# Spreading the first loads of a two-layer decoder over three DMA queues

## The chip, the cores and the metric

The kernel runs on one core of a Trainium2 chip. The metric is the device time of one execution in microseconds (us), as the median of several executions. Engines go by the profile's short names: PE is TensorE (PEld its weight loads), ACT is ScalarE, DVE is VectorE, POOL is GpSimd, SP is SyncE. SP, ACT and POOL can issue DMA transfers; an issue on SP or ACT is a step of that engine's instruction stream, and the transfers themselves run on 16 DMA engines that all three share.

## The reference

The input is x, 512 tokens of 1024 features in float32. Two layers follow each other, and each does this:

```python
x = x + 0.5 * swiglu(rms_norm(x, ffn1_norm[l]), ffn1_w_gate[l], ffn1_w_up[l], ffn1_w_down[l])
h = rms_norm(x, mix_norm[l])
a, g, q, k, v = jnp.split(h @ w_in[l], splits, axis=-1)
conv_out = conv_module(a, g, conv_w[l], conv_b[l], conv_norm[l])
...
x = x + jnp.concatenate([conv_out, diff_out], axis=-1) @ w_out[l]
x = x + 0.5 * swiglu(rms_norm(x, ffn2_norm[l]), ffn2_w_gate[l], ffn2_w_up[l], ffn2_w_down[l])
```

swiglu(h) is (silu(h @ w_gate) * (h @ w_up)) @ w_down with 2816 hidden features. The change concerns how x, the first gate and up weights and the layers' small parameters get into the core at the very start. None of the arithmetic is touched.

## The kernel before, in words

The activations are kept with features on the 128 partitions: x has KT = 8 feature tiles x[0] to x[7], each 128 x 512 (256 KB, and it stays on the chip through both layers). To multiply in float32 on TensorE, each operand is split into two parts, hi and lo, of the type float32r, and each product is three matmuls: hi by hi (line 163), hi of the weights by lo of x (166), lo of the weights by hi of x (167). For weights, ScalarE makes hi (line 100; for the very first piece VectorE, line 98) and VectorE makes lo (line 101). For x, a Prep object makes acth on ScalarE (line 262) and actl on VectorE (line 263), with the norm's gain, a column of the parameter tile pars[l], multiplied in; the row statistics come later, from squares on ScalarE (line 271) that GpSimd adds up (line 275).

The first stretch is written out by hand. The parameters of both layers (79.5 KB each) are issued on ScalarE's queue (line 179). Then an activation that needs nothing loads the activation table (line 184), and IDLE = 9 matmuls without use keep TensorE busy (line 187). Four weight tiles of the first feed-forward, gate and up of hidden tiles 0 and 1, are loaded in three pieces each on SP's queue, between the feature tiles that they are multiplied with: columns for feature tile 0 (64 KB), for tiles 1 to 3 (192 KB), for tiles 4 to 7 (256 KB). On SP the issues thus stand in this order: x[0], four first pieces, x[1], four second pieces, x[2], x[3], x[4], four third pieces, x[5], x[6], x[7]. The text calls the pieces first, second and third pieces. lead_products multiplies them feature tile by feature tile: for each k the four products, so that TensorE can begin when one feature tile and the first pieces are there. After that come 20 more hidden tiles, loaded as whole weight tiles by SP, some with sums that GpSimd's queue accumulates (line 141).

The tile framework decides the rest. It plans the order of instructions on each engine ahead of the run, from the order of the program text and a model of durations; only instructions passed through keep_in_program_order are pinned behind what was written before them on their engine. It also adds the semaphores. The code does not show them, but the trace lists for each DMA issue which semaphore it will count up and which it waits for.

The rest of the parameters' use: make_scalars (lines 505 to 538) makes small scaled copies of both layers' parameters on GpSimd. pars[1] has its first reader there.

Of the kernel before, what the change touches and what calls it, by code (L numbers as in the profile page):

```python
# [19 lines left out]
DEPTH = 2  # L20
# [47 lines left out]
def trunk(ctx: ExitStack, tc: tile.TileContext, xt, par, lamv, relb, onehot,  # L68
          gu1, dn1, wag, wqkv, wout, gu2, dn2, out):
    nc = tc.nc  # L70
# [10 lines left out]
    def f32(ap):  # L81
        return ap.bitcast(F32)
# [3 lines left out]
    def bank(tag, name):  # L86
        return psum.tile([P, 512], F32, tag=tag, name=name, bufs=BANKS[tag])
# [8 lines left out]
    def parts_of(raw, hi, lo, eng=None, first=False):  # L96
        if first:
            V.tensor_scalar(hi, raw, 1.0, None, op0=ALU.mult)
        else:
            S.activation(hi, raw, AF.Copy)  # L100
        (eng or V).tensor_tensor(out=lo, in0=raw, in1=f32(hi), op=ALU.subtract)  # L101
# [68 lines left out]
    x = act.tile([P, KT, SEQ], F32, tag="x", name="x")  # L170
# [3 lines left out]
    pars = []  # L174
    for l in range(DEPTH):
        pt = const.tile([P, NPAR], F32, tag=f"par{l}", name=f"par{l}")
        pars.append(pt)
    for l in range(DEPTH):
        nc.scalar.dma_start(pars[l], par[l])

    ones_r = const.tile([P, P + SPACE], F32R, tag="ones_r", name="ones_r")[:, :P]
    V.memset(f32(ones_r), 1.0)

    tc.keep_in_program_order(S.activation(const.tile([P, 1], F32, tag="warm", name="warm"), f32(ones_r[:, :1]), AF.Copy))
    ps = bank("tp", "ps_idle")
    for n in range(IDLE):
        mm = T.matmul(ps, ones_r, ones_r.unsqueeze(1).broadcast_to([P, NT, P]), start=True, stop=True)
# [2 lines left out]
    lead = [[ring("wraw"), ring("whi"), ring("wlo")] for _ in range(4)]  # L190
    for k0, k1 in ((0, 1), (1, 4), (4, KT)):
        h = slice(k0 * P, k1 * P)
        nc.sync.dma_start(x[:, k0, :], xt[k0])
        for n, (raw, hi, lo) in enumerate(lead):
            nc.sync.dma_start(raw[:, h], gu1[0, n // 2, n % 2][:, h])
            parts_of(raw[:, h], hi[:, h], lo[:, h], first=k0 == n == 0)
        for k in range(k0 + 1, k1):
            nc.sync.dma_start(x[:, k, :], xt[k])
    lead = [[tuple(t[1:]) for t in lead[2 * m : 2 * m + 2]] for m in range(2)]
    ident = const.tile([P, P], F32, tag="ident", name="ident")  # L200
# [731 lines left out]
```

## Time and profile before

| what | us |
|---|---|
| median of 3 runs | 1796.49 (1795.98 to 1796.54) |
| time of the profiled execution | 1796.31 |
| its span, first to last instruction | 1794.5 |
| first useful matmul starts | 4.98 |
| last piece of x lands | 17.26 |
| lead_products ends on TensorE, about | 28.7 |

The span is what the profile covers; the time of the same execution is 1.8 us longer. All positions below are microseconds from the start of the span. The first transfers, with the moment of issue and of landing:

| transfer | queue | issued | landed |
|---|---|---|---|
| par[0] | ACT | 0.72 | 4.00 |
| par[1] | ACT | 1.16 | 4.41 |
| x[0] | SP | 0.73 | 3.80 |
| first pieces 1 to 4 | SP | 1.17, 1.64, 2.10, 2.58 | 4.21, 4.60, 5.14, 5.34 |
| x[1] | SP | 3.05 | 6.35 |
| second pieces 1 to 4 | SP | 4.01, 4.39, 4.86, 5.34 | 6.88, 8.36, 9.23, 10.03 |
| x[2], x[3], x[4] | SP | 5.82, 6.29, 6.76 | 11.19, 11.87, 12.52 |
| third pieces 1 to 4 | SP | 7.24, 7.71, 8.37, 9.25 | 13.20, 13.88, 14.56, 15.23 |
| x[5], x[6], x[7] | SP | 10.05, 11.20, 11.88 | 15.91, 16.58, 17.26 |

An issue occupies its engine for 0.33 to 0.45 us. In the same stretch ScalarE issues the two parameter transfers until 1.61, loads its table from 1.65 to 2.93, runs the warming activation until 3.14, and makes the first acth from 4.02.

### The profile page before, as it was taken

To read this page: it belongs to the slowest core of one execution; us is meant where nothing else is said; L and a number is where in the kernel's file an instruction comes from. 1 tells how busy PE (TensorE), PEld (TensorE's weight loads), DVE (VectorE), ACT (ScalarE), POOL (GpSimd) and SP (SyncE) were. 2 spreads that over 40 slices of the span, in tenths; PEclk is the share of its full clock that TensorE was granted. 3 is DMA by queue.
4 is the path that set the end of the run, shared out by engine and by line. 5 is a ranking of instruction groups with operands and counts; after the bars stand their busy time and mean duration, and the time that the engine had idled before them with its cause. 6 is when DMAs were issued, how large, how long until landed. Compare 5 with 4: busy or idle time off the path is not lost.

```text
span 1794.5 us, 28356 instructions
## 1 busy us (share of the span) xinstructions
PE 1784.6 (99%) x10845; PEld 1590.1 (89%) x10845; DVE 1211.1 (67%) x1863; ACT 896.1 (50%) x1482; POOL 653.6 (36%) x460
## 2 busy tenths in 40 slices
PE   9999999999999999999999999999999999999999
PEld 7899899888788899899888998998887888998997
DVE  6976477568867867477576765765788587673762
ACT  6555265445744456256433643654558354552651
POOL 4242232269843132133102312412797331322420
PEclk9999999999999999999999999999999999999999
DMA  7466476323212366466333654663231133664651
GB/s 243 107 179 183 108 181 176 118 94 94 71 48 83 94 165 188 106 171 189 105 94 98 171 167 120 177 179 118 71 114 51 48 106 91 166 178 112 180 150 59
DMA packets 111721, 231.24 MB, mean 129 GB/s; under 512 B 12151, under 2 KB 33414, under 8 KB 111584
## 3 DMA queue, kind: packets, MB, share of 16 engines
q1 hardware_dynamic: 91488, 191.93, 33.4%
q0 software_dynamic: 19808, 37.33, 12.5%
q8 instruction: 85, 1.39, 0.3%
q14 instruction: 52, 0.43, 0.1%
q10 hardware_dynamic: 288, 0.16, 0.0%
HBM read 227.26 MB, written 3.42 MB: 129 GB/s over the span
## 4 chain that ended last, share of the span: by engine, by line
PE 96%; DVE 2%; issue 1%; ACT 1%; DMA 0%; SPq 0%; ACTq 0%; DVEq 0%
PE ps_pair L384 38%; PE ps_d L166 9%; PE ps_d L163 9%; PE ps_d L167 9%; PE ps_pair L167 5%; PE ps_pair L166 5%; PE ps_pair L163 5%; PE ps_pair L596 2%; PE ps_pair L597 2%; PE ps_pair L598 2%; PE ps_out L163 1%; PE ps_out L166 1%; PE ps_sc L714 1%; PE ps_out L167 1%; DVE actl L263 1%; PE ps_v L628 1%
## 5 line engine op out<-in xcount | busy, mean ns | idle before, releaser
L100 ACT ACTIVATE whi<-wraw 128x1024 fp32r<-128x1024 f32 (+2 forms) x599 | 465.9, 802 | 609.5 <-PE ps_pair L384 225.7
L101 DVE TENSOR_TENSOR wlo<-wraw,whi 128x512 fp32r<-128x512 f32 (+2 forms) x556 | 526.0, 968 | 212.6 <-ACT whi L100 208.4
L384 PE MATMUL ps_pair<-acth,wlo 128*128 128x256 f32 x1088 | 308.5, 284 | 0.0
L384 PE MATMUL ps_pair<-actl,whi 128*128 128x256 f32 x1088 | 308.5, 284 | 0.0
L384 PE MATMUL ps_pair<-acth,whi 128*128 128x256 f32 x1088 | 308.4, 283 | 0.0
L166 PE MATMUL ps_d<-hl,whi 128*128 128x512 f32 x704 | 274.2, 390 | 0.0
L167 PE MATMUL ps_d<-hh,wlo 128*128 128x512 f32 x704 | 273.4, 390 | 0.0
L163 PE MATMUL ps_d<-hh,whi 128*128 128x512 f32 x704 | 268.7, 390 | 0.0
L384 PE MATMUL ps_pair<-th,wlo 128*128 128x256 f32 x816 | 231.3, 283 | 0.0
L384 PE MATMUL ps_pair<-tl,whi 128*128 128x256 f32 x816 | 231.2, 283 | 0.0
L384 PE MATMUL ps_pair<-th,whi 128*128 128x256 f32 x816 | 231.2, 283 | 0.0
L146 POOL TENSOR_TENSOR wraw<-wraw 128x512 f32<-128x512 f32 x68 | 101.8, 1497 | 339.5 <-DMA wraw<-in_gu 272.2
L141 POOL DMA_DIRECT2D wraw<-in_gu x68 | 82.0, 1207 | 392.4 <-DMA wraw<-in_gu 228.6
L384 PEld LDWEIGHTS ps_pair<-acth,whi 128*128 128x128 f32 x1088 | 209.1, 192 | 0.3
L384 PEld LDWEIGHTS ps_pair<-actl,whi 128*128 128x128 f32 x1088 | 209.0, 192 | 0.3
L384 PEld LDWEIGHTS ps_pair<-acth,wlo 128*128 128x128 f32 x1088 | 209.1, 192 | 0.0
L480 DVE SCALAR_TENSOR_TENSOR x<-ps_d,x 128x512 f32<-128x512 f32 x96 | 64.7, 689 | 179.6 <-PE ps_d L167 179.3
L166 PE MATMUL ps_pair<-actl,whi 128*128 128x512 f32 x448 | 175.0, 391 | 0.3
L163 PE MATMUL ps_pair<-acth,whi 128*128 128x512 f32 x448 | 174.4, 394 | 0.5 <-ACT whi L100 0.3
L167 PE MATMUL ps_pair<-acth,wlo 128*128 128x512 f32 x448 | 174.5, 391 | 0.0
L384 PEld LDWEIGHTS ps_pair<-tl,whi 128*128 128x128 f32 x816 | 156.7, 192 | 0.7
L384 PEld LDWEIGHTS ps_pair<-th,whi 128*128 128x128 f32 x816 | 156.7, 192 | 0.6
(176 smaller groups left out, 3268.9 us busy)
## 6 DMA issues: line engine op xcount, KB each, us to landing
wraw<-in_gu SPq DMA_DIRECT2D x208, 256.0 KB, 4.0
wraw<-in_gu SPq DMA_DIRECT2D x104, 512.0 KB, 3.7
wraw<-in_gu POOLq DMA_DIRECT2D x68, 512.0 KB, 5.7
wraw<-in_wqkv SPq DMA_DIRECT2D x24, 512.0 KB, 3.7
wraw<-in_dn SPq DMA_DIRECT2D x84, 128.0 KB, 3.1
wraw<-in_dn SPq DMA_DIRECT2D x32, 256.0 KB, 3.1
wraw<-in_wag SPq DMA_DIRECT2D x16, 512.0 KB, 3.6
wraw<-in_wout SPq DMA_DIRECT2D x16, 512.0 KB, 3.6
```

The costliest lines, as they stand in the source:

```text
L100: S.activation(hi, raw, AF.Copy)
L101: (eng or V).tensor_tensor(out=lo, in0=raw, in1=f32(hi), op=ALU.subtract)
L141: nc.gpsimd.dma_start(two.rearrange("p (b c) -> p b c", b=2), u[:, h[0]].unsqueeze(1).broadcast_to([P, 2, 512]), accum_op=ALU.add)
L146: G.tensor_tensor(more[:, h[0]], two[:, h[1]], whole[:, h[0]], op=ALU.add)
L163: first = T.matmul(ps, wh, xh, start=start, stop=False)
L166: T.matmul(ps, wh, xl, start=False, stop=False)
L167: T.matmul(ps, wl, xh, start=False, stop=stop)
L384: mm = T.matmul(ps, l, r, start=first and i == j == 0, stop=False, skip_group_check=True)
L480: V.scalar_tensor_tensor(x[:, m, :], ps, 0.5, x[:, m, :], op0=ALU.mult, op1=ALU.add)
L596: T.matmul(ps[n], xh[:, t], wh, start=k == 0, stop=False)
L597: T.matmul(ps[n], xh[:, t], wl, start=False, stop=False)
L598: T.matmul(ps[n], xl[:, t], wh, start=False, stop=k == KT - 1)
```

## The change

Of the two parameter transfers only the first layer's stays on ScalarE's queue; the second layer's is issued by GpSimd. ScalarE's queue also takes x[1], straight behind par[0], and x[2] and x[3], which the program text places behind the warming activation. SP's queue keeps x[0], x[4] to x[7] and all weights, in the same order as before.

```diff
-    for l in range(DEPTH):
-        nc.scalar.dma_start(pars[l], par[l])
+    nc.scalar.dma_start(pars[0], par[0])
+    nc.scalar.dma_start(x[:, 1, :], xt[1])
+    nc.gpsimd.dma_start(pars[1], par[1])
 
     ones_r = const.tile([P, P + SPACE], F32R, tag="ones_r", name="ones_r")[:, :P]
     V.memset(f32(ones_r), 1.0)
 
     tc.keep_in_program_order(S.activation(const.tile([P, 1], F32, tag="warm", name="warm"), f32(ones_r[:, :1]), AF.Copy))
+    for k in range(2, 4):
+        nc.scalar.dma_start(x[:, k, :], xt[k])
...
     for k0, k1 in ((0, 1), (1, 4), (4, KT)):
         h = slice(k0 * P, k1 * P)
-        nc.sync.dma_start(x[:, k0, :], xt[k0])
+        if k0 != 1:
+            nc.sync.dma_start(x[:, k0, :], xt[k0])
         for n, (raw, hi, lo) in enumerate(lead):
             nc.sync.dma_start(raw[:, h], gu1[0, n // 2, n % 2][:, h])
             parts_of(raw[:, h], hi[:, h], lo[:, h], first=k0 == n == 0)
-        for k in range(k0 + 1, k1):
+        for k in range(max(k0 + 1, 5), k1):
             nc.sync.dma_start(x[:, k, :], xt[k])
```

## The prediction

> **What bounds the kernel now.** I read four views: the page's busy shares, the chain that ended last in order of time, the busy time by windows of 5 us, and the timelines of the single engines over the first 13 us. The page and the chain first:
>
> ```profile
> span 1794.5 us, 28356 instructions
> PE 1784.6 (99%) x10845; PEld 1590.1 (89%) x10845; DVE 1211.1 (67%) x1863; ACT 896.1 (50%) x1482; POOL 653.6 (36%) x460
> ...
> PE 96%; DVE 2%; issue 1%; ACT 1%; DMA 0%; SPq 0%; ACTq 0%; DVEq 0%
> ```
>
> TensorE bounds the whole, and 96% of the chain is its work. The change touches only transfers issued in the first 13 us, so it can win only what TensorE loses there. The chain in order of time (start, us, what) shows how that stretch hangs together:
>
> ```profile
> 0.72 3.27 DMA par<-in_par
> 4.01 0.33 SPq L195
> 5.82 5.37 DMA x<-in_xt
> 11.21 0.73 ACT acth L262
> 11.99 1.20 PE ps_pair L163 x4
> ```
>
> The reader sees a chain that runs from the first layer's parameters (issued 0.72, landed 4.00) to an issue on SP at 4.01, along SP's queue to the third feature tile (x[2]) issued at 5.82, which lands only at 11.19; ScalarE makes its acth from 11.21, and TensorE goes on at 11.99. Why does an issue on SP follow a landing of ScalarE's? The semaphores of the issues answer it: the transfers of SP and ScalarE take turns on eight semaphores, and one that takes a semaphore again waits until its last user has landed. The ninth transfer (weights, 4.01) follows the landing of par at 4.00; later ones follow in the same way (issue 11.20 on the landing at 11.19, 11.88 on 11.87, 12.54 on 12.52). So **eight transfers are in flight at most**, and a slot counts as much as an issue.
>
> TensorE's timeline shows the price (start, us; with the idle time and its releaser):
>
> ```profile
> 4.63 0.52 PE L187 MATMUL ps_idle<-ones_r 128*128 128x512 f32 x1
> 4.98 0.62 PE L163 MATMUL ps_pair<-acth,whi 128*128 128x512 f32 x2
> ...
> 8.23 0.39 PE L166 MATMUL ps_pair<-actl,whi 128*128 128x512 f32 x1
> 8.96 0.50 PE L163 MATMUL ps_pair<-acth,whi 128*128 128x512 f32 x1 [0.34 <-ACT whi L100]
> ...
> 9.83 0.50 PE L163 MATMUL ps_pair<-acth,whi 128*128 128x512 f32 x1
> ...
> 11.20 0.62 PE L167 MATMUL ps_pair<-acth,wlo 128*128 128x512 f32 x2
> 11.99 1.20 PE L163 MATMUL ps_pair<-acth,whi 128*128 128x512 f32 x4 [0.16 <-ACT acth L262]
> ```
>
> An undisturbed matmul of this shape follows the one before after 0.23 us (7.08, 7.31, 7.54). The busy times overlap and hide most waiting, so I go by starts. What exceeds 0.23 between 8.23 and 12.32 is 0.49 + 0.11 (second weight piece, 8.96, and the slow restart behind it), 0.08 + 0.11 (third, 9.83), 0.10 (fourth, 10.63) and 0.32 + 0.11 (x[2], 11.99): **1.32 us in all, 0.43 of it from x[2]**. Before, between 4.98 and 5.92, another 0.26 goes; at 28.66 to 29.42 another 0.30, which is a chain of TensorE, ScalarE and VectorE and moves along with TensorE. Nothing else is lost: from 12.3 to 28.6 the 0.23 us rhythm holds. The most that any order of the loads could bring is thus about 1.9 us, 0.1% of the span.
>
> The windows (PE, PEld, DVE, ACT, POOL busy, clock, DMA share, GB/s) show what room the DMA engines have:
>
> ```profile
> 0.00:5.00 5.00, 3.96 (x10) 3.03 (x11) 0.90 (x5) 2.41 (x4) 2.32 (x14) 1.00 0.54 162
> 5.00:10.00 5.00, 4.67 (x19) 3.02 (x19) 3.19 (x8) 2.70 (x6) 3.58 (x9) 1.00 0.87 279
> 10.00:15.00 5.00, 4.84 (x20) 3.51 (x21) 3.96 (x7) 4.22 (x7) 0.00 (x0) 1.00 1.01 345
> 15.00:20.00 5.00, 5.00 (x23) 4.14 (x23) 3.72 (x6) 4.92 (x9) 0.86 (x1) 1.00 1.04 400
> ```
>
> They are half idle in the first 5 us and full from 10 us. Bytes moved into the first 5 us use free time; bytes moved into 5 to 10 us take most of it from others.
>
> **The change, part by part.**
>
> *Second layer's parameters to GpSimd.* They cost ScalarE's queue 0.45 us of issue and one of the eight slots. On GpSimd one more DMA issue appears; its rows are relb's at 0.73 us (1.58) and the large accumulating transfers' at 1.21 us. Behind it stand memsets and the identity, first used by TensorE at 31.5. The parameters' first reader is GpSimd's own product at 6.48; issued by 2 us with relb's 3.2 us to landing they are there by 5.2. Cost 0; with the cover gone it would be 1.2 us on GpSimd, which first feeds TensorE by the sums of squares (ready 30.2, used 31.5: 1.3 us to spare). Bounds 0 and 0.
>
> *x[1] as ScalarE's second issue.* It takes the place of the parameters' issue (0.41 to 0.45 us, so the table load at 1.65 stays) and leaves at about 1.2, not 3.05. With its 3.3 us it lands near 4.6, not 6.35. TensorE's second feature waits on weights (6.88), not on it, so this wins nothing by itself. It competes with the first weight pieces: 262 KB against 79.5 KB before, 0.18 MB more, 0.45 us at 400 GB/s at the very worst. The first product is covered until 4.98 by the warming matmuls (last start 4.63), while its last operand, acth, is ready at 4.74. I take 0; bounds 0 and +0.4.
>
> *x[2] and x[3] behind the table load on ScalarE.* Two issues of 0.43 us are 0.86. ScalarE idles for 0.88 between the warming activation (over at 3.14) and its first acth at 4.02, which waits for par. They fit, **if neither waits for a slot**. With 0.43 us each and slots free they land near 6.5 and 7.2, not 11.19 and 11.87. The 0.43 us of x[2] goes. I take -0.43; bounds -0.43 and 0. The wait is the edit's risk: priced below.
>
> *SP's queue without three issues.* x[1] stood ahead of the second weight pieces, x[2] and x[3] behind them. SP could issue the pieces 0.47 us earlier, but they then need slots that x[2] and x[3] have taken, and 0.52 MB more moves beside them (1.3 us at 400 GB/s). The 0.89 us lost to the pieces is bounded by -0.89 (they arrive in TensorE's rhythm) and +0.9 (the first piece lands at 8.2, 1.3 later; TensorE would start on it at 8.9, not 8.00). The nearest rows, 0.87 DMA share and 0.47 us of issue saved, lie on both sides; half of the gain is what I take: -0.45.
>
> *Later.* The stop at 29.08 and the sums of squares follow TensorE and x[7]; the latter lands at 17.26 in a full stream, and the same bytes begun earlier end earlier. 0.
>
> **Sum:** -0.43 - 0.45 = -0.88, about -0.9 us. The profiled execution took 1796.31 (span 1794.5 and 1.8 around it), so 1795.4; the median of the three runs stands 0.18 higher, so the forecast is **1795.6**. A measurement of this kernel tells about 0.2% (3.6 us) from no change, so this counts as the same.
>
> Here a rule of the Trainium skill speaks against the change: "DMA: Bandwidth & Descriptors", section "Issuing engines are not separate DMA queues", says that transfers of all issuing engines interleave on the same 16 DMA engines, and that spreading them saves only the issue time. The rows agree from 10 us on (share 1.01) and leave room before 5 us (0.54). By the rule my -0.88 would shrink to about 0, the first rival.
>
> **The rivals.**
>
> 1. *Shared engines: nothing is won.* The early bytes of x[2] and x[3] push back the second weight pieces by as much as x[2] is early. For it: the share of 0.87 in 5 to 10 us; against: 0.54 before. Place: the wait at 8.96. Some 0.4 us lost there pay for the 0.43 won: 1796.5.
>
> 2. *All is won.* The pieces come in rhythm as well and the early 0.26 shrinks: -1.3 to -1.9, so 1794.6 to 1795.2. Against it: the pieces land 1.48, 0.87 and 0.80 apart, and TensorE needs them 0.69 apart.
>
> 3. *Slower: ScalarE blocked at its own issue.* If x[2] or x[3] draws a used semaphore, ScalarE stands still until a predecessor lands (par 4.00, or x[1] about 4.6), issues only then, and the first acth (due 4.02) with all weight splits behind it comes 0.45 to 1.3 us later. It decides as soon as both issues are beyond the eighth slot, since then the loss (up to 1.3 at TensorE's first product) exceeds the 0.43 won; with the 0.89 kept by the pieces the kernel ends 0.5 to 1.3 us later, 1797.0 to 1797.8. For it: SP alone fills five slots by 2.6 us, ScalarE two by 1.6, so only one or two are left when the warming activation is over at 3.14. Against it: the issue order was planned, and the two may be planned ahead of the table load, with slots free.
>
> 4. *The planner orders later work otherwise.* The instruction order of each engine comes from a planning pass, not from the text alone, so a shifted start may change it far away, and x[2] may not even stand where the diff puts it. Against it: the two layers start from different states and still run alike. In the chain
>
> ```profile
> 459.39 2.58 PE ps_sc L714 x6
> ...
> 1350.25 2.58 PE ps_sc L714 x6
> ```
>
> the pieces lie 890.86 apart, as do the stops before them (500.20 and 1391.06 begin 1.53 us each). An order that did change might bring or cost some three such stops, over 3.6 us: 1792 or 1801.
>
> **How the numbers follow.** Forecast (-0.3 to -1.3) 0.44; all won 0.12; nothing won (within 0.3) 0.18; ScalarE blocked 0.12; replanned 0.14, of which 0.06 fast and 0.08 slow. The first four reach from 1794.6 to 1797.8 and hold 0.86; with the spread of the runs shown (the lowest lies 0.5 under the median) below that I give 1794.0 to 1797.8. Only the replanned cases leave the 0.2%: faster 0.06, same 0.86, slower 0.08.
>
> **What would show it.** Right: the chain of the changed kernel has no x transfer before TensorE's run; x[2] lands before 8 us; no stop near 12 us; TensorE leaves its first layer's warm part near 27.8 instead of 28.7, and all later pieces of the chain stand 0.9 earlier. Wrong: a gap on ScalarE in front of the issue of x[2] or x[3], the first product later than 4.98, second pieces landing later than 6.88, 8.36, 9.23 and 10.03, or distances between later pieces of the chain that differ from those of before.

## The result, and the profile after

The changed kernel takes 1798.72 us (median of 22 runs, 1796.94 to 1800.05), the kernel before 1796.09 (22 runs, 1795.40 to 1797.03). The ratio is 1.0015, 95% interval 1.0009 to 1.0022: slower by 2.6 us. That is inside the 0.2% that the forecast called the same, but outside its range (1794.0 to 1797.8) and on the other side of no change. The profiled execution of the changed kernel took 1800.05, the slowest of the 22, with a span of 1798.3.

From the page of the changed kernel, the span and the busy times:

```profile
span 1798.3 us, 28356 instructions
PE 1786.0 (99%) x10845; PEld 1592.1 (89%) x10845; DVE 1209.5 (67%) x1863; ACT 895.3 (50%) x1482; POOL 649.8 (36%) x461
```

Its chain in order of time (start, us, what), the start and one later piece that the prediction showed of before:

```profile
0.72 3.10 DMA par<-in_par
3.85 3.38 DMA wraw<-in_gu
7.22 0.69 ACT acth L266
7.96 1.22 PE ps_pair L163 x2
...
463.03 2.58 PE ps_sc L718 x6
...
1353.90 2.58 PE ps_sc L718 x6
```

The transfer of x[2] is gone from the chain, as forecast, but the first product now waits until 7.96, not 4.98. The two late pieces lie 890.87 apart (890.86 before), and the first of them stands 3.64 later (463.03 against 459.39). So the loss lies at the start, and the layers themselves did not change.

ScalarE's timeline of the changed kernel says why the first product is late (start, us; in brackets the idle time and its releaser):

```profile
0.72 0.42 ACTq L178 DMA_DIRECT2D par<-in_par  x1
1.17 0.45 ACTq L179 DMA_DIRECT2D x<-in_xt  x1
1.65 1.28 ACT L185 ACT_TABLE_LOAD   x1 [1.65 <-PEq L925]
1.72 0.87 ACTq L187 DMA_DIRECT2D x<-in_xt  x2
2.95 0.20 ACT L185 ACTIVATE warm<-ones_r 128x1 f32<-128x1 f32 x1
6.99 0.31 ACT L100 ACTIVATE whi<-wraw 128x128 fp32r<-128x128 f32 x1 [3.84 <-DMA wraw<-in_gu]
7.21 1.93 ACT L266 ACTIVATE acth<-x,par 128x512 fp32r<-128x512 f32 x3
```

Two things stand here. The first work after the warming activation is now a weight split (line 100), and only then the first acth; before, it was the other way round:

```profile
4.02 0.72 ACT L262 ACTIVATE acth<-x,par 128x512 fp32r<-128x512 f32 x1 [0.88 <-DMA par<-in_par]
4.65 0.29 ACT L100 ACTIVATE whi<-wraw 128x128 fp32r<-128x128 f32 x1
```

And the changed kernel's split stands still for 3.84 us for its transfer: the second of the first pieces, issued at 1.64 in both kernels, lands at 6.97 instead of 4.60. par had landed at 3.83 and x[0] at 3.60, so the first acth could have run at 3.85. (The chain names a weights transfer issued at 3.85 for this wait. ScalarE's own timeline, with the landing at 6.97 beside the split at 6.99, is the better witness.)

TensorE's timeline of the changed kernel, after the warming matmuls:

```profile
7.96 1.22 PE L163 MATMUL ps_pair<-acth,whi 128*128 128x512 f32 x2 [2.71 <-ACT acth L266]
8.98 0.63 PE L166 MATMUL ps_pair<-actl,whi 128*128 128x512 f32 x1
9.41 0.63 PE L167 MATMUL ps_pair<-acth,wlo 128*128 128x512 f32 x1
...
13.68 0.57 PE L163 MATMUL ps_pair<-acth,whi 128*128 128x512 f32 x1
14.08 0.39 PE L166 MATMUL ps_pair<-actl,whi 128*128 128x512 f32 x1
14.31 0.40 PE L167 MATMUL ps_pair<-acth,wlo 128*128 128x512 f32 x1
```

From here on, a product is one matmul. lead_products does 96 of them, so the 97th is the first of the third hidden tile.

Up to 13.68 the products follow each other after 0.43 us, from 14.08 on after 0.23. No wait stands between them; they are simply slow, as the warming matmuls are (0.43 apart). In the kernel before the fast rhythm was there from 4.98 on. The trace's record of TensorE's granted clock fits: it begins with full clock at 4.88 before and at 14.04 in the changed kernel. Ahead of that it is empty, and the 1.00 that a window view prints there is no measurement. So TensorE did not fall back to the slow rhythm while it was idle; it had not yet left it when it fell idle at 5.25.

The accounts: the first product 2.98 later; 14 steps between 7.96 and 14.08 that take 6.12 instead of 14 x 0.23 = 3.22, so 2.90; against that the stops of before between 4.98 and 12.32 are gone (0.26 + 1.32 = 1.58). That makes 4.3, and the 97th product starts 4.24 later (32.68, before 28.44). The stop of 0.30 at the third hidden tile is gone as well. The profiled execution is 3.74 over that of the kernel before; the medians differ by 2.6.

### The profile page after: what moved, and what is told of

Read it like the earlier page. It is cut to its first block, busy times and chain, and to the rows that moved or that the text cites. A ratio compares the mean times of both kernels' runs of the same rounds, so it can differ in the third digit from the quotient of the medians.

```text
span 1798.3 us, 28356 instructions
## 1 busy us (share of the span) xinstructions
PE 1786.0 (99%) x10845; PEld 1592.1 (89%) x10845; DVE 1209.5 (67%) x1863; ACT 895.3 (50%) x1482; POOL 649.8 (36%) x461
## 4 chain that ended last, share of the span: by engine, by line
PE 96%; DVE 2%; ACT 1%; issue 1%; DMA 0%; ACTq 0%; DVEq 0%
PE ps_pair L388 38%; PE ps_d L166 9%; PE ps_d L167 9%; PE ps_d L163 9%; PE ps_pair L166 5%; PE ps_pair L163 5%; PE ps_pair L167 5%; PE ps_pair L601 2%; PE ps_pair L600 2%; PE ps_pair L602 2%; PE ps_out L166 1%; PE ps_sc L718 1%; PE ps_out L167 1%; PE ps_out L163 1%; DVE actl L267 1%; PE ps_v L630 1%
```

## The experiments

Theory A: the transfers of x that now leave in the first 2.6 us share the DMA engines with the first weight pieces, which land late; ScalarE's planned order makes the first acth wait for such a piece; and TensorE, idle from 5.25 to 7.96, runs slowly for some 6 us after that. Rivals are named with each run. All kernels were timed in 11 runs each beside runs of the kernel before (its medians 1796.06 to 1796.27). Most of the ratio intervals below are about 0.0009 wide on either side and contain 1. So the verdicts rest on medians beside the spread of the runs, and on the traces.

**1. A longer cover.** The changed kernel with

```diff
-IDLE = 9
+IDLE = 21
```

> The changed kernel with 21 warming matmuls instead of 9 (the instruction order of ScalarE, SP and GpSimd is the same as in the changed kernel). Theory A (first pieces land late, the first product waits until 7.96, TensorE stands idle for 2.9 us in front of it, and its clock is then low for 5.7 us): the cover lasts to about 8.0, the first product still starts near 8.0, but the 13 products behind it follow each other after 0.23 us instead of 0.43, so the time falls by 2.6 us, to about 1796.1. Rival B (the loss lies in the loads alone, the slow products were going to wait for data anyway): the time stays at 1798.7, within 0.5.

Measured: 1797.31 (1797.09 to 1798.01), ratio to before 1.0005 (0.9996 to 1.0013). TensorE's timeline of this run:

```profile
7.85 0.73 PE L163 MATMUL ps_pair<-acth,whi 128*128 128x512 f32 x2
...
8.97 0.39 PE L167 MATMUL ps_pair<-acth,wlo 128*128 128x512 f32 x1
9.19 0.39 PE L166 MATMUL ps_pair<-actl,whi 128*128 128x512 f32 x1
```

The first product starts as late (7.85), but the fast rhythm is there (the record of the clock begins at 4.65), and the 97th product starts at 30.18, not 32.68. B falls. A's time is missed by 1.2: in the medians the cover is worth 1.4, not 2.6, since the size had been read off the one profiled execution of the changed kernel, its slowest. The spread shrinks from 3.1 us in 22 runs to 0.9 in 11. That points to the slow stretch as what makes the changed kernel's times scatter, but it is not shown.

**2. The second layer's parameters alone on GpSimd's queue.** The kernel before with

```diff
-    for l in range(DEPTH):
-        nc.scalar.dma_start(pars[l], par[l])
+    nc.scalar.dma_start(pars[0], par[0])
+    nc.gpsimd.dma_start(pars[1], par[1])
```

> The kernel before with one part of the change: the second layer's parameters are issued by GpSimd, x[1] to x[3] stay on SP. Theory A (the bytes of x[1] to x[3] are what delays the first pieces): as before, 1796.1 within 0.4, first product at 5.0, first piece 2 lands by 4.8. Rival C (GpSimd's transfer, whose packets take 0.35 us each, is what delays the first pieces): first piece 2 lands after 5.5 and the time rises by 1 to 2.6 us.

Measured: 1796.86 (1796.76 to 1797.36), ratio 1.0004 (0.9995 to 1.0013), 0.7 more than before in the medians; neither expectation fits. The first product starts at 5.05 and first piece 2 lands at 4.89, close to what A says. The loss is elsewhere: a step of 1.76 us at 28.57, where the kernel before has one of 0.42. Experiments 7 and 8 take it up. This run also shows that the slow rhythm needs no idle stretch: its matmuls follow each other without a stop from the first warming one on, and the record of the clock begins only at 6.87.

**3. x[1] alone on ScalarE's queue** (parameters on GpSimd, x[2] and x[3] back on SP). The changed kernel with

```diff
-    for k in range(2, 4):
-        nc.scalar.dma_start(x[:, k, :], xt[k])
...
-        for k in range(max(k0 + 1, 5), k1):
+        for k in range(max(k0 + 1, 2), k1):
```

> The changed kernel with x[2] and x[3] back on SP: only x[1] goes to ScalarE's queue (and the second layer's parameters to GpSimd's). ScalarE's order is then acth of x[0], acth of x[1], splits of first pieces 2 to 4. Theory A: 262 KB share the DMA engines with the first pieces, a third of the bytes of the full change, so first piece 2 lands 0.5 to 0.9 later (5.1 to 5.5), the first product still starts at 5.0 since piece 1 and x[0] are there, TensorE waits about 0.5 us behind it and wins 0.4 elsewhere: 1795.8 to 1796.8. Rival C (GpSimd's transfer): about as slow as the full change, over 1797.5.

Measured: 1796.62 (1796.54 to 1797.95), ratio 1.0002 (0.9993 to 1.0011), as A expected. First piece 2 lands at 5.57, TensorE stops for 0.86 at 5.05 and hardly again: the 97th product starts at 27.69, 0.75 earlier than before. That is nearly the gain that was forecast, but with x[2] and x[3] still on SP: the move of x[1] alone brought the second pieces and x[2] in time (x[2] lands at 9.79, not 11.19). A stop of 1.65 us at 27.91 eats the gain.

**4. x[2] and x[3] alone on ScalarE's queue** (parameters on GpSimd, x[1] on SP). The changed kernel with

```diff
-    nc.scalar.dma_start(x[:, 1, :], xt[1])
...
-        if k0 != 1:
-            nc.sync.dma_start(x[:, k0, :], xt[k0])
+        nc.sync.dma_start(x[:, k0, :], xt[k0])
```

> The changed kernel with x[1] back on SP: x[2] and x[3] go to ScalarE's queue (and the second layer's parameters to GpSimd's). ScalarE's planned order is acth of x[0], acth of x[1], split of first piece 2, acth of x[2], so the first product is not behind first piece 2. Theory A: 524 KB stand beside the first pieces, which land 1 to 2 us late, and x[1], needed by ScalarE ahead of the splits, lands after 7; the first product starts at 5.0 but TensorE then stops for about 2 us and its clock may fall: 1797.0 to 1799.0. Rival D (the planned position of the split in front of the first acth is the whole loss, not the bytes): 1795.5 to 1796.3.

Measured: 1797.32 (1796.32 to 1798.04), ratio 1.0005 (0.9996 to 1.0014). First piece 2 lands at 6.14. TensorE starts at 5.05, stops for 1.48 and then runs in 0.43 us steps until 10.1 (clock record from 10.07). The expectation misread the planned order (ScalarE's second acth is that of x[2], landed 5.00, not of x[1]), but the time is the one A gave. D falls: the first acth is not held up here (3.95), and the kernel is still slower.

**5. The first acth ahead of the splits.** The changed kernel with the first acth and actl traced before the weights, and the splits held behind it on ScalarE:

```diff
+    nc.sync.dma_start(x[:, 0, :], xt[0])
+    a0 = S.activation(acth[:, 0, :], x[:, 0, :], AF.Copy, scale=pars[0][:, 0:1])
+    V.scalar_tensor_tensor(
+        actl[:, 0, :], x[:, 0, :], pars[0][:, 0:1], f32(acth[:, 0, :]), op0=ALU.mult, op1=ALU.subtract
+    )
...
-            parts_of(raw[:, h], hi[:, h], lo[:, h], first=k0 == n == 0)
+            with tc.issue_after(a0.ins):
+                parts_of(raw[:, h], hi[:, h], lo[:, h], first=k0 == n == 0)
```

> The changed kernel with the first acth traced ahead of the weight splits and the splits held behind it on ScalarE; all transfers as in the changed kernel. Theory A (bytes): first piece 2 still lands near 6.9, so the first product starts at 5.0, TensorE does the three products of piece 1 and then waits until about 7.3; it ends its lead stretch 0.7 to 1.3 us earlier than the changed kernel: 1797.3 to 1798.2. Rival D (the split planned ahead of the first acth is the whole loss): the 2.9 us of idle time and the slow clock go, 1795.5 to 1796.3.

Measured: 1797.68 (1797.01 to 1798.24), ratio 1.0007 (0.9998 to 1.0016). The first product starts at 5.05; first piece 2 lands at 6.51 and TensorE stops for 1.85. D falls: the order is worth 1.0 of the 2.6. The lateness of the piece and the slow rhythm behind the stop (until 10.4) remain.

**6. x[1] to x[3] issued behind the first acth.** Experiment 5 with

```diff
+    with tc.issue_after(a0.ins):
+        for k in range(1, 4):
+            nc.scalar.dma_start(x[:, k, :], xt[k])
```

in place of their earlier issues.

> The changed kernel with the first acth ahead, and with the issues of x[1], x[2] and x[3] on ScalarE held behind it, so that they leave at about 4.0 to 5.0 and not at 1.2 to 2.6. Theory A: the first pieces land by 5.6 as with the parameters alone, the first product starts at 5.0, no stop of more than 0.6 us follows, and TensorE reaches the third hidden tile 0.3 to 1.0 us earlier than before; there the squares planned in front of its split cost 1.0 to 1.6 us, as in the two runs with a part of the change (1.5 us lost at 28.6 and 27.9): 1796.2 to 1797.2. Rival F (three queues cost by themselves, wherever the transfers stand): as the full change, over 1798.

Measured: 1798.97 (1798.13 to 1799.91), ratio 1.0012 (1.0003 to 1.0021): outside what A expected. The first pieces land at 4.2 to 5.6, as A says, and TensorE starts at 5.05. But it stops for 2.11 us at 8.72. ScalarE's timeline of this run:

```profile
8.59 0.72 ACT L272 ACTIVATE acth<-x,par 128x512 fp32r<-128x512 f32 x1 [2.46 <-DMA x<-in_xt]
9.64 0.72 ACT L272 ACTIVATE acth<-x,par 128x512 fp32r<-128x512 f32 x1 [0.33 <-DMA x<-in_xt]
10.27 0.51 ACT L100 ACTIVATE whi<-wraw 128x384 fp32r<-128x384 f32 x1
```

The split of second piece 1, landed at 8.35, stands behind two acth that were planned ahead of it and waited for x[1] (8.56) and x[2] (9.62). Behind the first of the two it could have run at 9.31, not 10.27, so by this estimate the order is 1.0 of the 2.11. The rest goes to the late landings. SP issued nothing between 3.02 and 4.03, waiting for a semaphore, since the x transfers, which left from 4.04 on, had been given some of the eight; the DMA engines moved 108 GB/s from 4 to 6 us, where the kernel before has 269. So the changed kernel's fault is here again one stage later: a planned order on ScalarE that the landings do not keep. F cannot be ruled out by this run alone; experiments 2, 3 and 4, which issue on all three queues too and end at 1796.6 to 1797.3, speak against it.

**7 and 8. Who stops TensorE at the third hidden tile?** Experiments 3 and 2, each with the last of the eight squares traced between the two splits of that tile:

```diff
-        for k in range(KT):
+        for k in range(KT - 1):
             pr.squares(k, pin=True)
...
+                    if lead and m == 2:
+                        w = [chunk(gu[m, 0])]
+                        pr.squares(KT - 1, pin=True)
+                        w.append(chunk(gu[m, 1]))
```

> The run with x[1] alone on ScalarE's queue, and the last square traced between the two splits of the third hidden tile, so that ScalarE's order there is as in the kernel before (four squares, split, square) and not five squares and then the split. Theory G (the stop of 1.65 us at 27.9 in that run comes from the split waiting behind squares, which wait for GpSimd's sums): the stop shrinks to 0.3, the 0.75 us won up to 27.7 is kept, 1795.2 to 1795.6. Rival H (the stop is the weights' landing or the ring's release): it stays, 1796.6 within 0.3.

> The run with the second layer's parameters alone on GpSimd's queue, with the same edit of the last square. Theory G: the stop of 1.76 us at 28.6 shrinks to 0.3 and the time falls from 1796.9 to 1795.3 to 1795.7. Rival H: it stays at 1796.9 within 0.3.

Measured: 7: 1795.61 (1795.48 to 1795.77), ratio 0.9995 (0.9986 to 1.0004). 8: 1796.03 (1795.60 to 1798.12), ratio 0.9999 (0.9990 to 1.0008). They are 1.0 and 0.8 us faster than without the edit. The first fits G, the second comes out 0.3 slower than expected. The step is back to 0.23 in 7, which is no stop, and to 0.39 in 8, so H falls. In the kernel before, ScalarE's order was four squares, split, square; in experiments 2 and 3 the planner put all squares first. VectorE's and GpSimd's timelines of experiment 3 show the price:

```profile
27.34 2.17 DVE L101 TENSOR_TENSOR wlo<-wraw,whi 128x1024 fp32r<-128x1024 f32 x1 [5.53 <-ACT whi L100]
```

```profile
24.40 4.03 POOL L277 TENSOR_TENSOR ssum<-ssum,sq 128x512 f32<-128x512 f32 x3
```

and of experiment 7:

```profile
26.90 1.23 DVE L101 TENSOR_TENSOR wlo<-wraw,whi 128x1024 fp32r<-128x1024 f32 x1 [5.14 <-ACT whi L100]
```

```profile
27.53 1.75 POOL L277 TENSOR_TENSOR ssum<-ssum,sq 128x512 f32<-128x512 f32 x1 [0.52 <-ACT sq L273]
```

In 3 the lo part (the subtraction of line 101) starts at 27.34 beside GpSimd's last sum (until 28.43) and takes 2.17 us; in 7 it starts 0.44 earlier, ahead of the last sum, and takes 1.23. So the stop is about 0.4 us of order on ScalarE and 0.9 of VectorE and GpSimd in each other's way. The same sum comes out elsewhere: in experiment 2 the subtraction takes 2.18, begun 1.10 before GpSimd's end, and in the kernel before 1.56, begun 0.48 before it; 1.08 is left each time. The Trainium skill, "SBUF — State Buffer", section "SBUF: two separate sides", calls the port that these two share an exclusive lock, held for a whole instruction; the trace agrees: 2.17 is the 1.09 until GpSimd's end and then most of the instruction's own 1.2.

**9. A shorter cover in the kernel before** (with the square placed as in 7, so that ScalarE's order stays):

```diff
-IDLE = 9
+IDLE = 2
```

> The kernel before with 2 warming matmuls instead of 9 (and the last square traced between the two splits of the third hidden tile, which keeps ScalarE's order as before); all transfers as before. Theory A (an idle stretch of TensorE ahead of the first product makes the products behind it follow after 0.43 us): with no matmul from 2.2 to 4.9 the first product starts at about 4.8, but up to 13 products run at 0.43 us; some of that lies in waits for the pieces that were there anyway (1.6 us in all before): the lead stretch ends 0.8 to 2.0 us later and the time is 1797.0 to 1798.2. Rival B (the slow products only fill waits for data): 1796.2 within 0.4.

Measured: 1796.52 (1795.98 to 1797.06), ratio 1.0002 (0.9993 to 1.0011): below A's range and within B's. The trace shows the mechanism all the same: 13 products from 4.64 to 10.36 follow after some 0.43 us, and the 97th starts at 29.35 instead of 28.44. Here most of the slow steps lie in time in which TensorE would have waited for pieces anyway. So slow steps cost only where the data are there, as in the changed kernel.

**10 and 11. A version from the findings.** The second layer's parameters go to the end of SP's first loads, and the square is placed as in 7. In 10 x[1] is on SP, in 11 on ScalarE.

```diff
-    nc.gpsimd.dma_start(pars[1], par[1])
...
+    nc.sync.dma_start(pars[1], par[1])
     lead = [[tuple(t[1:]) for t in lead[2 * m : 2 * m + 2]] for m in range(2)]
```

> A version from the findings: x[1] to x[3] on SP as before, the second layer's parameters issued by SP behind x[7], so that nothing stands beside the first pieces and a slot is free, and the last square traced between the two splits. Theory A: first piece 2 lands by 4.6, second piece 1 leaves at about 3.5, TensorE waits less before 9, the lead stretch ends 0.5 to 1.0 us earlier than before: 1795.2 to 1795.8. Rival I (GpSimd's copies of the late parameters delay the sums of squares, first used behind 30): 1796.2 or slower.

> The same with x[1] on ScalarE's queue, issued straight behind the first layer's parameters as in the change. Theory A: first piece 2 lands near 5.4 (262 KB beside it, no GpSimd transfer), TensorE waits about 0.5 us in its first feature tile, x[1] and the second pieces come in rhythm: 1795.2 to 1795.8, about as the run with x[1] and the parameters on GpSimd (1795.6). Rival C (GpSimd's transfer costs the first pieces something of its own): 0.3 to 0.6 us faster than that run, 1795.0 to 1795.3.

Measured: 10: 1797.12 (1796.75 to 1798.19), ratio 1.0006 (0.9997 to 1.0015). 11: 1796.68 (1796.37 to 1802.28), ratio 1.0006 (0.9997 to 1.0015). Misses for A as to time. First piece 2 lands at 4.68 and 5.26 and the 97th product starts at 28.25 and 28.24, 0.2 earlier than before. But GpSimd's copies of those parameters wait for the landing (17.07 in 10) and stand ahead of its sums. In 10 the sums begin at 19.93, not 19.14, meet VectorE's lo part, and TensorE stops for 1.42 at 28.47; in 11 it stops for 1.17 at 30.76, waiting for the sums themselves. Rival I holds. Rival C's time for 11 is missed as well.

**12. Both repairs that leave the transfers alone:** experiment 5 with IDLE = 19.

> The changed kernel with both repairs that leave its transfers alone: the first acth ahead of the splits (alone it brought the time from 1798.7 to 1797.7) and 19 warming matmuls (21 alone brought it to 1797.3). Theory A (both act on the same late start, and the landing of first piece 2 near 6.9 stays): the cover ends near 7.1, the products follow in the 0.23 us rhythm from there, the lead stretch ends 0.3 to 0.7 us earlier than with the cover alone: 1796.6 to 1797.1, still not faster than before. Rival J (the repairs act apart and add up, -1.0 and -1.4, so the bytes themselves cost nothing): 1796.2 or less.

Measured: 1796.82 (1796.54 to 1798.96), ratio 1.0005 (0.9996 to 1.0014). A's time is met, but not its mechanism: in the profiled execution first piece 2 landed at 5.99, the warming matmuls ran slowly until 7.0 (the last starts at 8.03), and the first product started at 8.26. So there the cover itself set the start, and not the piece. The products kept the 0.23 us rhythm. J's time is missed, but with a cover that outlasted the piece the run cannot tell whether the repairs would add up. What is left over before, about 0.8, cannot be split further with it.

The landings of first piece 2 (issued at 1.64 in every kernel, 64 KB) by what else was issued in the first 2.6 us:

| beside x[0], par[0] and the first pieces | KB | landed at |
|---|---|---|
| nothing more (10) | 0 | 4.68 |
| par[1] on ScalarE (before, 9) | 80 | 4.60, 4.69 |
| par[1] on GpSimd (2, 6, 8) | 80 | 4.89, 5.21, 5.35 |
| x[1] (11) | 256 | 5.26 |
| x[1], par[1] on GpSimd (3, 7) | 336 | 5.57, 5.56 |
| x[2], x[3], par[1] on GpSimd (4) | 592 | 6.14 |
| x[1] to x[3], par[1] on GpSimd (after, 1, 5, 12) | 848 | 6.97, 6.84, 6.51, 5.99 |

The more bytes, the later the piece; 256 KB more cost about 0.6 us (4.68 to 5.26, 5.56 to 6.14), which is what such a tile takes at 400 GB/s. The scatter of the last row is 1 us. The issuing queue counts for something too: the same 80 KB go with 4.60 and 4.69 on ScalarE's queue and with 4.89 to 5.35 on GpSimd's. So a part of rival C, 0.2 to 0.7 us of landing, stays open.

## Why the prediction was wrong

- **What bounds the kernel, and eight transfers in flight: right.** TensorE's start is where all of the difference lies, and an issue's wait for the last user of its semaphore showed again: in the changed kernel SP issues a transfer at 6.99, right behind the landing of first piece 2 at 6.97.
- **The room in the DMA engines: wrong, and the root of the rest.** The prediction read "half idle in the first 5 us" from a window of 5 us. The kernel before in windows of 2 us (last columns: clock, DMA share, GB/s) shows another picture:

```profile
0.00:2.00 2.00, 0.95 (x2) 0.83 (x3) 0.17 (x2) 0.35 (x1) 1.38 (x11) 1.00 0.02 5
2.00:4.00 2.00, 2.00 (x6) 1.55 (x5) 0.00 (x0) 1.13 (x2) 0.32 (x1) 1.00 0.91 291
4.00:6.00 2.00, 2.00 (x7) 1.21 (x7) 1.73 (x6) 1.43 (x4) 1.62 (x5) 1.00 0.88 269
```

  and of the changed kernel:

```profile
2.00:4.00 2.00, 2.00 (x6) 1.54 (x5) 0.00 (x0) 1.14 (x2) 1.31 (x9) 1.00 0.98 304
4.00:6.00 2.00, 1.25 (x3) 0.43 (x2) 0.52 (x2) 0.00 (x0) 1.33 (x5) 1.00 0.95 294
```

  The idle half is mostly the time before the first bytes move. From 2 to 6 us the engines were already at 0.91 and 0.88, and the change moved only some 0.08 MB more there (an estimate from the GB/s).
- **x[1] competes with the first pieces by 0.18 MB, at most 0.4: the failed step.** The sum let only x[1] stand beside the first pieces and put x[2] and x[3] at 3.14, after the warming activation. In the trace ScalarE issues them at 1.72 and 2.13, while its table load runs: the issues did not wait for it to end. So 0.79 MB of x stood beside the first pieces, first piece 2 landed 2.4 us later, and the first product came 2.98 later, where the sum has a bound of 0.4. The sentence that x[1] wins nothing by itself is wrong as well: experiment 3 differs from experiment 2 in x[1] alone and reaches the third hidden tile 0.65 earlier (27.69, not 28.34).
- **The first product is covered until 4.98: wrong.** It took for granted that ScalarE makes the first acth before the splits, as before. The planner moved a split ahead of it (experiment 5: 1.0 us), and the cover ended before the data came. The slow steps around an idle TensorE were no term of the sum at all (experiment 1: 1.4 us), although the warming matmuls stand 0.43 apart in the trace of before.
- **-0.43 for x[2] and -0.45 for the pieces: not shown for this change.** x[2] landed at 7.18, near the forecast, and behind its first product the changed kernel has no stop (1.58 us gone). But it reaches the second feature tile only at 12.82, and by then all second pieces (10.03) and x[2] (11.19) had landed in the kernel before too. Experiment 3 shows that a gain of this size was there to be had, by way of x[1] alone.
- **"Later: 0": wrong in kind, without harm here.** Where TensorE started in time, the planner's order mattered: with all squares ahead of a split, 1.4 us were lost at the third hidden tile (experiments 2, 3, 7, 8). The changed kernel has the same order but is too late to meet that stop.
- **The rivals.** The third had the right sign and engine, ScalarE held up by a transfer, but the wrong wait: no semaphore of its own issue, but a split planned ahead of the first acth. What it named against itself, that the two issues may be planned early with slots free, came close to what happened and was the harm. The fourth expected replanning far away in the layers; it came in the first 30 us. The first (nothing won, 1796.5) was nearer than the forecast, but 2.2 short of the measured time. The Trainium skill's rule behind it, "DMA: Bandwidth & Descriptors", section "Issuing engines are not separate DMA queues", fits the table of landings, where transfers of all three queues delay each other; by it alone the time would have stayed. That a small urgent transfer is delayed by large ones from another queue, and that this costs time, is what the runs add.

## What to carry to other kernels

At the start of this kernel, what decides is how many bytes move beside the small first pieces, largely whichever queue issues them. Move a large transfer forward only behind the small ones that the first work needs. Look at the DMA share in windows that leave out the time before the first byte. An earlier arrival also changes a planned order. A split ahead of its turn, and a stop that comes while TensorE is still in its slow rhythm, can both cost more than the wait that was removed.

Of the kernels tried, experiment 7 (x[1] alone on ScalarE, parameters on GpSimd, the last square moved) has the lowest median, 1795.61; all its 11 runs lie below the median of before (1796.27), but the interval of its ratio (0.9986 to 1.0004) leaves open whether it is faster.

## What the runs showed of the hardware

- A DMA issue on ScalarE goes out while the engine still loads its table (issue at 1.72, load from 1.65 to 2.93).
- TensorE's first matmuls follow each other after 0.43 us and later ones after 0.23. The trace's record of the granted clock begins where the fast rhythm does: between 4.12 and 7.21 us in the ten runs whose TensorE had been idle for at most 0.2 us at a time until then, and between 10.07 and 14.04 in the four with an earlier idle stretch of 0.8 to 2.7 us (the changed kernel, experiments 4, 5 and 9). Once there, the fast rhythm stayed, also over the stop of 2.11 us in experiment 6. A window view prints a clock of 1.00 in the slow stretch too, where the record is empty; the distance between starts shows the state. The Trainium skill, "TensorE: Matmul & The Clock Gate", section "Part 1: The HAM clock gate (the "warmup" mystery)", describes a half-rate state that only some 3.4 us of sustained work in a free-running window lift; the trace agrees in kind: the fast rhythm came 3.1 to 6.2 us after the first warming matmul in the ten runs, 6.1 us after the first product in the changed kernel, 6.0 us in experiment 9.
- A subtraction on VectorE (128x1024, float32) that takes 1.21 to 1.23 us alone took 2.17 us when it began beside a sum on GpSimd.
